# Hybrid GLA/FoX decoder block: where the split v of the GLA output step is kept, and in which order the steps of its four heads are given out

## The chip, the cores and the metric

The kernel runs on one core of one Trainium2 chip. The metric is the device time of one execution in microseconds (us). The kernel before took 1661.32 us, the median of three runs (1660.44 to 1662.15).

## The reference

One decoder layer on 256 tokens of width 2048, all in float32. Only the first part bears on the change:

```
q, k, v, r  = parts of x @ w_in            # GLA: 4 heads, dk 256, dv 512
o_t  = sum over s <= t of  A[t, s] * v_s   # A: q.k with a data-dependent decay
o    = o * rsqrt(mean(o*o) + eps) * gain   # per head, over its 512 columns
o    = o * silu(r)
y_gla = o @ w_branch_gla
```

FoX attention, two merge gates `sigmoid(x @ w)` (2048 columns each), the output projection, LayerNorm, a gated MLP, a second LayerNorm and a per-layer embedding follow or stand beside it.

## The kernel before

**Number format.** Every float32 matrix product is done as three products of rounded parts: `hi` is the operand copied by ScalarE (ACT) into the fast float32r format, `lo` is the remainder `x - hi`, subtracted by VectorE (DVE). The products hi·hi, hi·lo and lo·hi are added in PSUM. So each weight matrix costs a DMA (`raw`), an ACT copy (`hi`, L112) and a DVE subtraction (`lo`, L220) before TensorE (PE) can use it.

**Weights.** Units of 1 MB pass in a fixed order through `prep` (two DMAs on SyncE's (SP's) queue into a ring of five buffers, then `hi` and `lo`, six buffers each), three units ahead of use. SP's order is the program's order; the order on the other engines is made by a scheduler when the program is built. It places an instruction as early as its inputs and a free buffer allow.

**Stages in time.** Value and early projections (`fv`, `psfq`, `psfk`), GLA q and k and the matrices A (`at`), 20 of 32 merge-gate products (`merge_gate`, tile `psm`), the GLA values v (`gv`) and the output gate r (`gr`) by `s_half`, then the remaining twelve gate products n = 20 to 31, and then the branch products (`psa` with the GLA output `oT`, `psb` with FoX). Each gate product is 16 pairs of products: 512 columns with `hi` (L287) and 256 with `lo` (L289).

**The GLA output step.** `o_gen` is a generator whose pieces are given out between the products of those twelve gates: from n = 21 on, `pull(1)` is called after the pairs 3 and 11 of each gate. For each head h it does

- `split(h)`: v is split into hi and lo (tile `vs`, 8 KB per partition, taken from the pool of fifteen 8 KB buffers, `s8`), and A into `ath` and `atl`;
- `product(h)`: nine products of 512 columns (L956) into two PSUM banks (`go`), the sum of squares on ACT (L959), the power -0.5 on GpSimd (POOL, L963), and the scaled and gated result `og` on DVE (L965);
- `turn(h)`: eight transposes of `og` on PE (L974, tile `gt`, the same two PSUM banks, pool `pmx`), then their split into the 8 KB tile `oT` (ACT L112, DVE L992).

Between the pieces stand yields, and the heads follow one another:

```
for h in range(H):
    split(h); yield; yield
    product(h); yield; yield
    turn(h); yield
```

**Buffers.** While the twelve gates run, the fifteen 8 KB buffers hold x transposed (4), the FoX output (2), A (1), the gate results (4) and v with r (4, freed head by head). `vs` and `oT` need buffers of the same pool. A second, smaller space, the pool `ec`, holds constants of the early stages (masks, a scan reset, a matrix of ones, the norm gain `gnb`); it is closed after the twelve gates. Of these only `gnb` is still used in the stage `gr` (L922).

Later tiles take the 8 KB buffers as they come free. The next is `td`, 1 MB of weights that `park_gen` loads during the branch products (L160) to prepare them ahead; its DMA stands in SP's queue between the loads of `raw`, which wait behind it.

Of the kernel before, what the change touches and what calls it, by code (L numbers as in the profile page):

```python
# [9 lines left out]
F32 = mybir.dt.float32  # L10
F32R = mybir.dt.float32r
# [3 lines left out]
ALU = mybir.AluOpType  # L15
# [4 lines left out]
P = 128  # L20
# [4 lines left out]
H = 4  # L25
# [19 lines left out]
PSM1 = 20  # L45
# [27 lines left out]
def tile_block(ctx: ExitStack, tc: tile.TileContext, wu, wfv, wpp, xT_in, x_in, pT_in, wlr,  # L73
               chan, gnorm, lng, ident_in, mask_in, cmask_in, out):
    nc = tc.nc
# [13 lines left out]
    sm = ctx.enter_context(tc.tile_pool(name="sm", bufs=2))  # L89
    early = ctx.enter_context(ExitStack())  # L90
    ec = early.enter_context(tc.tile_pool(name="ec", bufs=1))
    pmm = ctx.enter_context(tc.tile_pool(name="pmm", bufs=6, space=PSUM))
    pmx = ctx.enter_context(tc.tile_pool(name="pmx", bufs=2, space=PSUM))
    dr = ctx.enter_context(tc.tile_pool(name="dr", bufs=1, space=DRAM))

    def s8(shape, dt=F32, name=None):
        return big.tile(shape, dt, tag="S8", name=name)
# [4 lines left out]
    def t2(name):  # L102
        return sm.tile([P, 512], F32, tag="t2", bufs=6, name=name)

    def mmtile(name):
        return pmm.tile([P, 512], F32, tag="mm", name=name)

    def mxtile(name):
        return pmx.tile([P, 512], F32, tag="mx", name=name)

    def copy(o, i, scale=1.0):
        return nc.scalar.activation(o, i, AF.Copy, bias=0.0, scale=scale)  # L112
# [115 lines left out]
    def unit(ahead=3):  # L228
        u = n_used[0]
        n_used[0] += 1  # L230
        while n_prep[0] < min(NU, u + ahead):
            prep()
        return ready.pop(u)
# [19 lines left out]
    ident = cst.tile([P, P], F32, name="ident")  # L253
    mask = ec.tile([P, 8, 256], U8, name="mask")
    cmask = ec.tile([P, 256], F32, name="cmask")
    gnb = ec.tile([P, 512], F32, name="gnb")
    reset = ec.tile([P, 256], F32, name="reset")
    ones = ec.tile([P, P], F32R, name="ones")
    gSt = ec.tile([P, 256], F32R, name="gSt")
# [20 lines left out]
    def w_unit(ps, hi, lo, act, kts, first, last, hoff=0, tick=None):  # L280


        n = len(kts)
        for i, kt in enumerate(kts):
            a = act[kt // 4]
            w0 = (hoff + i) * P
            nc.tensor.matmul(ps, lhsT=hi[i // 8 if hoff == 0 else 0][:, w0 % 1024:w0 % 1024 + P],  # L287
                             rhs=a[:, kt % 4, :], start=first and i == 0, stop=False)
            nc.tensor.matmul(ps[:, 256:512],  # L289
                             lhsT=lo[i // 8 if hoff == 0 else 0][:, w0 % 1024:w0 % 1024 + P],  # L290
                             rhs=a[:, kt % 4, 0:256], start=False, stop=last and i == n - 1)
            if tick is not None:
                tick(i)
# [15 lines left out]
    def comb(ps, o, scale=1.0):  # L309
        tmp = t1("tmp")  # L310
        copy(tmp, ps[:, 256:512], scale)
        a = ps[:, 0:256]
        if len(o.shape) == 3:
            a, tmp = [v.rearrange("p (t n) -> p t n", t=2) for v in (a, tmp)]
        if scale == 1.0:
            nc.vector.tensor_tensor(o, a, tmp, ALU.add)
        else:
            nc.vector.scalar_tensor_tensor(o, a, scale, tmp, ALU.mult, ALU.add)
# [19 lines left out]
    def pull(n, gens=mixers):  # L338
        for _ in range(n):
            while gens:  # L340
                try:
                    next(gens[0])
                    break
                except StopIteration:
                    gens.pop(0)
# [92 lines left out]
    for u in range(8):  # L438
        hi, lo = fvu[u]
        for j in range(2):  # L440
# [8 lines left out]
            for t, i, c in seq:  # L449
                o, n = fch[c]  # L450
                w, x = prods[t][i]
# [34 lines left out]
    for t in range(2):  # L486
        for c, (o, n) in enumerate(fch):
            n = min(n, 1024 - o)
# [146 lines left out]
    for n in range(16):  # L635
        h, j = n // 2, n % 2
# [89 lines left out]
    for n in range(16):  # L726
        nm, dst, sc = (("q", gq, 1.0 / 16.0), ("k", gk, 1.0))[n // 2 % 2]
        h, c = n // 4, n % 2
# [157 lines left out]
    def merge_gate(n, tick=None):  # L886
        hi, lo = unit()
        ps = mmtile(f"psm{n}")
        w_unit(ps, hi, lo, xT, range(16), True, True, tick=tick)
        dst = sg[n // 8][:, n % 8, :]  # L890
        comb(ps, dst)
        nc.scalar.activation(dst, dst, AF.Tanh, bias=0.0, scale=0.5)
# [11 lines left out]
        pull(1)  # L904


    vg = [s8([P, 2, 2, 512], name=f"vg{h}") for h in range(H)]

    for nh in range(2):
# [26 lines left out]
    def o_gen():  # L936
        parts, ogs = {}, {}

        def split(h):
            vs = s8([P, 2, 2, 512], F32R, name=f"vs{h}")  # L940
            copy(vs[:, 0], vg[h][:, 0])
            nc.vector.tensor_tensor(vs[:, 1], vg[h][:, 0], vs[:, 0].bitcast(F32), ALU.subtract)
            ah, al = [sm.tile([P, 384], F32R, tag="t2", bufs=6, name=n) for n in ("ath", "atl")]
            copy(ah, at[h])
            nc.vector.tensor_tensor(al, at[h], ah.bitcast(F32), ALU.subtract)
            parts[h] = vs, ah, al

        def product(h):
            vs, ah, al = parts.pop(h)
            for t in range(2):  # L950
                po = mxtile(f"go{h}_{t}")
                ks = ((0, 0),) if t == 0 else ((256, 0), (128, 1))
                mm = [(x[:, o:o + P], vs[:, i, s, :]) for o, s in ks
                      for x, i in ((ah, 0), (ah, 1), (al, 0))]
                for j, (x, v) in enumerate(mm):
                    nc.tensor.matmul(po, lhsT=x, rhs=v, start=j == 0, stop=j == len(mm) - 1)  # L956
                sq = t2("sq")
                st = sm.tile([P, 2], F32, tag="gst", name="gst")
                nc.scalar.activation(sq, po, AF.Square, bias=0.0, scale=1.0,  # L959
                                     accum_out=st[:, 0:1])  # L960
                nc.vector.tensor_scalar(st[:, 0:1], st[:, 0:1], 1.0 / 512, RMS_EPS,
                                        ALU.mult, ALU.add)
                nc.gpsimd.tensor_tensor(st[:, 1:2], st[:, 0:1], mhalf, ALU.pow)  # L963
                og = ogs[h, t] = t2("og")
                nc.vector.scalar_tensor_tensor(og, po, st[:, 1:2], vg[h][:, 1, t, :],  # L965
                                               ALU.mult, ALU.mult)

        def turn(h):
            oT[h] = s8([P, 4, 512], F32R, name=f"oT{h}")
            for t in range(2):  # L970
                og = ogs.pop((h, t))
                pt = mxtile(f"gt{h}_{t}")
                for i in range(4):
                    nc.tensor.transpose(pt[:, i * P:i * P + P], og[:, i * P:i * P + P], ident)  # L974
                split_T(pt, oT[h], t)

        for h in range(H):
            split(h)
            yield
            yield  # L980
            product(h)
            yield
            yield
            turn(h)
            yield

    def split_T(pt, dst, t):

        p3 = pt.rearrange("p (k t) -> p k t", t=P)
        hi = dst[:, :, t * P:t * P + P]  # L990
        copy(hi, p3)
        nc.vector.tensor_tensor(dst[:, :, 256 + t * P:256 + t * P + P], p3,  # L992
                                hi.bitcast(F32), ALU.subtract)

    mixers.append(o_gen())


    for n in range(PSM1, 32):
        merge_gate(n, lambda i: pull(1) if i in (3, 11) and n > PSM1 else None)
    while mixers:  # L1000
        pull(1)
    early.close()
# [6 lines left out]
    for n in range(16):  # L1009
# [27 lines left out]
        i = WO_C.index(pair)  # L1037
# [242 lines left out]
    for n in range(NF):  # L1280
# [23 lines left out]
        if pair in DN_S[0]:  # L1304
            if j == 0:
                yp = t2("yp").rearrange("p (k t) -> p k t", t=S)
            h = yp[:, j, :]
        else:
            h = y
# [266 lines left out]
```

## Time and profile before

| | |
|---|---|
| median of three runs | 1661.32 us |
| profiled execution | 1661.22 us |
| its span (first to last instruction) | 1659.4 us |
| PE busy | 1652.1 us |
| weight loads on PE (PEld) | 1434.6 us |
| DVE busy | 1307.9 us |
| ACT busy | 899.8 us |
| POOL busy | 71.2 us |
| granted PE clock | 1.0 |

All times in the views are from the span's start. The profiled execution's time is 1.8 us longer than its span. The ends of products on PE are modelled, and products overlap; so what a product costs PE is read from its start to the start of the next one. In the view in order of time a row gives start, duration, engine, line, operation, output and inputs, the number of merged instructions, and in brackets the idle time before it with what ended it.

### The profile page before, as it was taken

How to read it: one execution, taken by the hardware profiler on the slowest of the kernel's cores; microseconds unless marked ns; L12 is line 12 of the kernel's file. 1: busy time of each engine (PE TensorE's matmuls, PEld its weight loads, DVE VectorE, ACT ScalarE, POOL GpSimd, SP SyncE). 2: the span in 40 equal slices, each digit the busy share in tenths (PEclk: the TensorE clock that was granted, in tenths of full speed). 3: DMA queues.
4: the chain of work that ended last, by engine and by line, in shares of the span. 5: the costliest groups of instructions: out<-in, count | busy, mean ns of one | idle time of the engine just before them, and what ended most of it. 6: DMA issues, size and time to landing. Idle time of an engine off the chain costs nothing.

```text
span 1659.4 us, 24382 instructions
## 1 busy us (share of the span) xinstructions
PE 1652.1 (100%) x8917; PEld 1434.6 (86%) x8917; DVE 1307.9 (79%) x1983; ACT 899.8 (54%) x1314; POOL 71.2 (4%) x210
## 2 busy tenths in 40 slices
PE   9999999999999999999999999999999999999998
PEld 9988888888888888888898888888888888888887
DVE  7666877888889767888987877777777778988774
ACT  6655555555555654455575455555545556556543
POOL 0100000000000000000010101100111000000000
PEclk9999999999999999999999999999999999999999
DMA  8755555546566556878856877778677679898554
GB/s 322 254 165 169 170 175 173 185 158 201 199 205 203 186 187 250 307 241 306 314 172 204 274 269 268 265 243 290 241 263 253 237 268 339 288 363 312 177 187 156
DMA packets 103432, 391.61 MB, mean 236 GB/s; under 512 B 11736, under 2 KB 13024, under 8 KB 96400
## 3 DMA queue, kind: packets, MB, share of 16 engines
q1 hardware_dynamic: 98448, 363.83, 64.3%
q0 software_dynamic: 4864, 26.23, 4.2%
q8 instruction: 70, 1.15, 0.3%
q14 instruction: 50, 0.41, 0.1%
HBM read 362.74 MB, written 27.27 MB: 235 GB/s over the span
## 4 chain that ended last, share of the span: by engine, by line
PE 98%; DVE 1%; ACT 0%; issue 0%; POOL 0%; POOLq 0%; DVEq 0%; ACTq 0%
PE dn L792 10%; PE psu L287 10%; PE psg L287 9%; PE psm L287 7%; PE pg L333 5%; PE psu L289 5%; PE psg L289 5%; PE gv L792 4%; PE gr L792 4%; PE wo L792 4%; PE psm L289 4%; PE dn_p L792 3%; PE psa L287 3%; PE fv L452 3%; PE psfk L287 2%; PE psk L287 2%
## 5 line engine op out<-in xcount | busy, mean ns | idle before, releaser
L220 DVE TENSOR_TENSOR lo<-raw,hi 128x1024 fp32r<-128x1024 f32 x490 | 595.0, 1220 | 192.8 <-ACT hi L112 190.7
L112 ACT ACTIVATE hi<-raw 128x1024 fp32r<-128x1024 f32 x490 | 516.0, 1057 | 380.3 <-issue 143.5
L287 PE MATMUL psu<-x1T,hi 128*128 128x512 f32 x688 | 240.4, 392 | 0.0
L287 PE MATMUL psg<-x1T,hi 128*128 128x512 f32 x672 | 234.8, 392 | 0.0
L289 PE MATMUL psu<-x1T,lo 128*128 128x256 f32 x688 | 192.3, 280 | 0.0
L289 PE MATMUL psg<-x1T,lo 128*128 128x256 f32 x672 | 187.8, 280 | 0.0
L287 PE MATMUL psm<-xT,hi 128*128 128x512 f32 x512 | 181.4, 396 | 0.0
L287 PEld LDWEIGHTS psu<-x1T,hi 128*128 128x128 f32 x688 | 129.2, 188 | 27.6
L287 PEld LDWEIGHTS psg<-x1T,hi 128*128 128x128 f32 x672 | 126.2, 188 | 27.0
L289 PE MATMUL psm<-xT,lo 128*128 128x256 f32 x512 | 143.3, 280 | 0.0
L289 PEld LDWEIGHTS psu<-x1T,lo 128*128 128x128 f32 x688 | 130.6, 190 | 0.0
L289 PEld LDWEIGHTS psg<-x1T,lo 128*128 128x128 f32 x672 | 127.6, 190 | 0.0
L287 PEld LDWEIGHTS psm<-xT,hi 128*128 128x128 f32 x512 | 96.2, 188 | 19.7
L792 PE MATMUL dn<-hi,hC 128*128 128x512 f32 x368 | 102.3, 389 | 0.0
L289 PEld LDWEIGHTS psm<-xT,lo 128*128 128x128 f32 x512 | 97.1, 190 | 0.2
L112 ACT ACTIVATE hi_b<-raw 128x512 fp32r<-128x512 f32 x78 | 65.3, 841 | 53.5 <-DMA raw<-in_wu_dram 19.8
L112 ACT ACTIVATE hi_t<-raw 128x1024 fp32r<-128x1024 f32 x48 | 51.0, 1063 | 75.5 <-DVE raw L148 51.1
L287 PE MATMUL psa<-oT,hi 128*128 128x512 f32 x256 | 89.8, 392 | 0.0
L194 DVE TENSOR_TENSOR lo_b<-raw,hi_b 128x512 fp32r<-128x512 f32 x78 | 73.7, 952 | 15.4 <-ACT hi_b L112 15.3
L792 PEld LDWEIGHTS dn<-hi,hC 128*128 128x128 f32 x368 | 69.0, 188 | 14.4
L289 PE MATMUL psa<-oT,lo 128*128 128x256 f32 x256 | 71.6, 280 | 0.0
L333 PE MATMUL pg<-hi,x2T 128*128 128x512 f32 (+1 forms) x256 | 69.7, 380 | 0.0
(366 smaller groups left out, 3199.5 us busy)
## 6 DMA issues: line engine op xcount, KB each, us to landing
raw<-in_wu_dram SPq DMA_DIRECT2D x553, 512.0 KB, 5.1
td<-in_wu_dram SPq DMA_DIRECT2D x15, 1024.0 KB, 8.5
td<-td POOLq DMA_DIRECT2D x15, 1024.0 KB, 6.5
td<-td SPq DMA_DIRECT2D x15, 1024.0 KB, 8.2
hS<-sd SPq DMA_DIRECT2D x21, 512.0 KB, 8.2
fvraw<-in_wfv_dram SPq DMA_DIRECT2D x13, 524.0 KB, 6.6
sd<-hs POOLq DMA_DIRECT2D x24, 256.0 KB, 5.7
lnb<-in_lng_dram SPq DMA_DIRECT2D x4, 1024.0 KB, 10.3
```

What stands on the lines that cost most here:

```text
L112: return nc.scalar.activation(o, i, AF.Copy, bias=0.0, scale=scale)
L194: nc.vector.tensor_tensor(lo, src, hi.bitcast(F32), ALU.subtract)
L220: i = nc.vector.tensor_tensor(lo, raw, hi.bitcast(F32), ALU.subtract)
L287: nc.tensor.matmul(ps, lhsT=hi[i // 8 if hoff == 0 else 0][:, w0 % 1024:w0 % 1024 + P], rhs=a[:, kt % 4, :], start=first and i == 0, stop= ...
L289: nc.tensor.matmul(ps[:, 256:512], lhsT=lo[i // 8 if hoff == 0 else 0][:, w0 % 1024:w0 % 1024 + P], rhs=a[:, kt % 4, 0:256], start=False, ...
L333: nc.tensor.matmul(bs[j][:, 0:m], lhsT=x, rhs=v[:, o:o + m], start=first and i == 0, stop=last and i == 2)
L452: nc.tensor.matmul(fbk[t][c][:, 0:n], lhsT=x, rhs=w[:, o:o + n], start=kt == 0 and i == 0, stop=kt == 15 and i == 2)
L792: nc.tensor.matmul(ps, lhsT=x, rhs=w, start=todo[id(ps)] == total[id(ps)], stop=todo[id(ps)] == 1)
```

## The change

- The pool `ec` first holds `gnb` alone. All other early constants go to a second pool, `ec2`, in the space behind it, and this pool is closed before the values stage; a third pool, `ec3`, is opened in the same space.
- `split(h)` no longer takes an 8 KB buffer. The hi part of v (`vh`, 4 KB) and one half of its lo part (`vl`, 2 KB) lie in `ec3`, in one buffer each; the other half of the lo part lies in a 2 KB buffer of the ring `t2` (six buffers, which `ath`, `atl`, `og` and the squares use too). The subtraction is made in two instructions of 512 columns instead of one of 1024.
- The order of the pieces: a new head begins every four pulls, its product two pulls after its split, and its transposes three pulls after its product (before: every five pulls, two, and two). The transposes of a head thus come after the split of the next one.
- The condition of the pulls is written in another way and holds for the same gates and pairs.

```diff
     ec = early.enter_context(tc.tile_pool(name="ec", bufs=1))
+    gnb = ec.tile([P, 512], F32, name="gnb")
+    first_ = ctx.enter_context(ExitStack())
+    ec = first_.enter_context(tc.tile_pool(name="ec2", bufs=1))
...
-    gnb = ec.tile([P, 512], F32, name="gnb")
...
+    first_.close()
+    ec = early.enter_context(tc.tile_pool(name="ec3", bufs=1))
     vg = [s8([P, 2, 2, 512], name=f"vg{h}") for h in range(H)]
...
         def split(h):
-            vs = s8([P, 2, 2, 512], F32R, name=f"vs{h}")
-            copy(vs[:, 0], vg[h][:, 0])
-            nc.vector.tensor_tensor(vs[:, 1], vg[h][:, 0], vs[:, 0].bitcast(F32), ALU.subtract)
+            vh = ec.tile([P, 2, 512], F32R, tag="vh", name=f"vh{h}")
+            copy(vh, vg[h][:, 0])
+            vl = [ec.tile([P, 512], F32R, tag="vl", name=f"vl{h}"),
+                  sm.tile([P, 512], F32R, tag="t2", bufs=6, name="vl1")]
+            for t in range(2):
+                nc.vector.tensor_tensor(vl[t], vg[h][:, 0, t], vh[:, t].bitcast(F32),
+                                        ALU.subtract)
+            vs = [(vh[:, t], vl[t]) for t in range(2)]
...
-                mm = [(x[:, o:o + P], vs[:, i, s, :]) for o, s in ks
+                mm = [(x[:, o:o + P], vs[s][i]) for o, s in ks
...
-        for h in range(H):
-            split(h)
-            yield
-            yield
-            product(h)
-            yield
-            yield
-            turn(h)
+        for k in range(19):
+            for f, o in ((turn, 5), (product, 2), (split, 0)):
+                h, r = divmod(k - o, 4)
+                if r == 0 and 0 <= h < H:
+                    f(h)
             yield
...
-        merge_gate(n, lambda i: pull(1) if i in (3, 11) and n > PSM1 else None)
+        merge_gate(n, lambda i: pull(1) if i in (3, 11) and 2 * n + i // 8 > 2 * PSM1 + 1 else None)
```

## The prediction

> **What bounds the kernel now.** I read the page's busy times first, then who waited for whom on PE, then PE's order of time where those waits lie.
>
> ```profile
> PE 1652.1 (100%) x8917; PEld 1434.6 (86%) x8917; DVE 1307.9 (79%) x1983; ACT 899.8 (54%) x1314; POOL 71.2 (4%) x210
> ```
>
> PE is busy in all but 7.3 us of the span of 1659.4. So the number of PE instructions and PE's waits set the time; work on DVE or ACT counts only where PE waits for it. The whole list of PE's waits has four rows (us in total, times, longest):
>
> ```profile
> PE warm_ps L122 <- DVE warm L119: 1.2, 1, 1.2
> PE gt L974 <- DVE og L965: 0.7, 2, 0.4
> PE gt L974 <- DVE gst L961: 0.4, 1, 0.4
> PE go L956 <- DVE atl L945: 0.4, 1, 0.4
> ```
>
> The first is the start of the program. The other three belong to the GLA output step: 1.5 us in four places. That understates the loss, since the modelled end of a product reaches past the start of the next. I therefore count from start to start. What an undisturbed product takes:
>
> ```profile
> 551.90 0.39 PE L287 MATMUL psm<-xT,hi 128*128 128x512 f32 x1
> 552.13 0.28 PE L289 MATMUL psm<-xT,lo 128*128 128x256 f32 x1
> 552.25 0.40 PE L287 MATMUL psm<-xT,hi 128*128 128x512 f32 x1
> ```
>
> 0.23 us for 512 columns, 0.12 for 256; a pair of a gate product takes 0.35, a gate of 16 pairs 5.55. Against that, the places where PE stood:
>
> ```profile
> 549.12 0.63 PE L956 MATMUL go<-vs,ath 128*128 128x512 f32 x2
> 550.18 0.50 PE L956 MATMUL go<-vs,atl 128*128 128x512 f32 x1 [0.43 <-DVE atl L945]
> 550.52 0.62 PE L956 MATMUL go<-vs,ath 128*128 128x512 f32 x2
> ...
> 607.00 0.73 PE L956 MATMUL go<-vs,ath 128*128 128x512 f32 x2
> 607.56 0.28 PE L289 MATMUL psm<-xT,lo 128*128 128x256 f32 x1
> ...
> 610.68 0.40 PE L287 MATMUL psm<-xT,hi 128*128 128x512 f32 x1
> 611.51 0.66 PE L974 MATMUL gt<-ident,og 128*128 128x128 f32 x4 [0.43 <-DVE gst L961]
> ...
> 612.36 0.28 PE L289 MATMUL psm<-xT,lo 128*128 128x256 f32 x1
> 613.05 0.66 PE L974 MATMUL gt<-ident,og 128*128 128x128 f32 x4 [0.41 <-DVE og L965]
> ...
> 619.70 0.39 PE L287 MATMUL psa<-oT,hi 128*128 128x512 f32 x1
> 620.39 0.66 PE L974 MATMUL gt<-ident,og 128*128 128x128 f32 x4 [0.30 <-DVE og L965]
> ```
>
> Head 0 at 549.12: two products took 1.06 instead of 0.45 and the next 0.34 instead of 0.23, together **0.72 lost**. Heads 2 and 3: 0.83 - 0.23 = 0.60, 0.69 - 0.12 = 0.57 and 0.69 - 0.23 = 0.46, together **1.63 lost**. At 607.00 the products of head 2 are torn apart: 0.56 instead of 0.45, **0.11 lost**. Each return from transposes to products costs a little too:
>
> ```profile
> 557.45 1.04 PE L974 MATMUL gt<-ident,og 128*128 128x128 f32 x8
> 558.24 0.48 PE L287 MATMUL psm<-xT,hi 128*128 128x512 f32 x1
> 558.56 0.28 PE L289 MATMUL psm<-xT,lo 128*128 128x256 f32 x1
> ```
>
> 0.32 instead of 0.23, so 0.09. Heads 0 and 1 return once each, heads 2 and 3 twice each, because their transposes come in fours: six returns. Everything the change can win on PE lies in these lines; behind them PE has no gap:
>
> ```profile
> 622.06:750.00 127.94, 127.94 (x741) 113.13 (x740) 105.27 (x177) 62.53 (x95) 2.72 (x5) 1.00 0.75 268
> ```
>
> (stretch, length, then the busy time of PE first.) So what is won before 622 stays won, if nothing new makes PE wait.
>
> **Why heads 2 and 3 are late.** By the pulls, split 2 is given out in gate n = 26 and split 3 in n = 28. The trace has them here (ACT, then DVE, then the results):
>
> ```profile
> 605.88 1.06 ACT L112 ACTIVATE vs<-vg 128x1024 fp32r<-128x1024 f32 x1
> ...
> 607.00 1.21 DVE L942 TENSOR_TENSOR vs<-vg,vs 128x1024 fp32r<-128x1024 f32 x1
> ...
> 610.70 0.75 DVE L965 SCALAR_TENSOR_TENSOR og<-go,gst,vg 128x512 f32<-128x512 f32 x1 [0.73 <-POOL gst L963]
> ```
>
> The gates begin at 536.64 (the end of the last `gr` product) and take 5.55 us each; a head costs PE nine products at 0.23, eight transposes in 0.79 (557.45 to 558.24) and the return, 3.0 together. With two heads done, n = 31 begins at 536.64 + 11 x 5.55 + 2 x 3.0 = 603.7, so split 2 stands in the last gate. Neither engine was too busy for it: what was missing is the 8 KB buffer, which came free only when the last gate had read the first part of x. After that the chain product, square, power, `og`, transposes, `oT` has only the rest of one gate and the first branch product beside it, and PE waits.
>
> **The change, part by part.**
>
> *Split v out of the 8 KB pool: heads 2 and 3.* `vh` and half of `vl` take the space of constants that were last read before the values stage; that space is free from then on. Each has one buffer, so split h+1 waits for product h; by the new order it stands two pulls, one gate, behind it. All four products and transposes then lie between gates n = 22 and n = 29 with gates beside them, and the three waits of 1.63 and the torn product of 0.11 go. Four whole groups of transposes return four times instead of six: 0.18 less. **Sum -1.92.**
>
> *What is late next for a head:* its `og`. Product to transposes is now three pulls, at least 8.3 us. In the trace head 2's products ended near 610, its `og` began at 610.70, and the transposes that waited for the second half began at 613.05: about 3 us are needed. Covered.
>
> *The split subtraction.* One instruction of 1024 columns becomes two of 512:
>
> ```profile
> L942 DVE TENSOR_TENSOR vs<-vg,vs 128x1024 fp32r<-128x1024 f32 x4 | 4.9, 1218 | 0.5 <-ACT vs L112 0.5
> L928 DVE TENSOR_TENSOR vg<-vg,gr 128x512 f32<-128x512 f32 x4 | 2.5, 679 | 0.0
> ```
>
> 2 x 679 - 1218 = 140 ns more on DVE per head, 0.56 us in all, beside PE work: 0, except for head 0 (next). The Trainium skill, "VectorE: DVE Perf Modes", section "The TRN2 errata — SBUF-src ops pay a fixed extra latency per instruction", speaks against this edit: a large tile pays the fixed part once, small ones each time. Its formula (N + 151)/0.96 gives 691 and 1224 ns, so an estimate of 158 ns more per head; the rows agree within some 20 ns, and by page or row the sum is the same.
>
> *Head 0's wait, now 0.72.* Its product stands where it stood (pull 2, 549.12). It needs `atl`, the last of a row of DVE work, and in the changed program one half of `vl` stands directly before `atl`, 0.61 us from start to start for such an instruction. Against that the whole `vs` of head 0 leaves DVE's queue before it, since `vh` and the first half of `vl` can be made right after the values stage:
>
> ```profile
> 518.40 1.22 DVE L942 TENSOR_TENSOR vs<-vg,vs 128x1024 fp32r<-128x1024 f32 x1
> ...
> 523.16 1.23 DVE L194 TENSOR_TENSOR lo_t<-raw,hi_t 128x1024 fp32r<-128x1024 f32 x1 [1.21 <-ACT hi_t L112]
> ...
> 531.15 1.23 DVE L220 TENSOR_TENSOR lo<-raw,hi 128x1024 fp32r<-128x1024 f32 x1 [1.62 <-ACT hi L112]
> ...
> 535.22 3.49 DVE L220 TENSOR_TENSOR lo<-raw,hi 128x1024 fp32r<-128x1024 f32 x3
> 538.63 2.47 DVE L928 TENSOR_TENSOR vg<-vg,gr 128x512 f32<-128x512 f32 x4
> ...
> 549.58 0.54 DVE L945 TENSOR_TENSOR atl<-at,ath 128x384 fp32r<-128x384 f32 x1
> ```
>
> From 538.63 to 549.58 DVE has no idle time (the bracket is empty in every row between), so `atl` moves as the row of 538.63 does. That row could have begun near 536.6, when the last `gr` products ended, but three subtractions lay ahead. They wait for weights: the transfers reuse the ring buffers that the subtraction at 523.16 and those after it free, and that one waited for ACT, which waited for DVE's differences behind `vs`. Without the 1.1 us that `vs` takes from the next start, this chain moves forward by 1.1 or more (its two waits for ACT can shrink as well), and at most by 2.0 (538.63 - 536.64). Needed for no wait: `atl` done by 549.57 (the start of the third product) instead of 550.18, with 0.61 more ahead of it: 1.22. Bounds: with no shift the wait grows to 0.72 + 0.61 = 1.33; with a shift of 1.22 or more it is 0. I take 0, because the shift's range is 1.1 to 2.0 and the remainder at its low end is 0.1. **-0.72.** By the page's 691 ns for that half, the need would be 1.30 instead of 1.22.
>
> *The early half.* `vh` (1.05 on ACT) and `vl` (0.68 on DVE) now run at the end of the first values half, among weight preparation. If they delayed a weight, PE would lose at most those 1.05; but units are prepared up to three ahead, a unit is 21 or 24 products of 0.23 there, about 5 us, and PE's list of waits has none in that stage. I take 0.
>
> *SP's queue.* The buffers of the later tiles change hands in another order. The first `td` waited for the last `atl` and left at
>
> ```profile
> 613.84 0.33 SPq L160 DMA_DIRECT2D td<-in_wu_dram  x1
> 617.28 0.33 SPq L216 DMA_DIRECT2D raw<-in_wu_dram  x1
> ```
>
> Now it waits for PE's reading of the first quarter of x in gate n = 31: that gate begins at 536.64 + 11 x 5.55 + 4 x 3.0 = 609.7, and four pairs later it is 611. The weight behind `td` left at 617.28, for reasons of its own ring. No new wait: 0. DMAs in number and size, and the work of ACT and POOL, are unchanged: 0.
>
> **Sum:** -1.92 - 0.72 = -2.6 of the profiled execution's 1661.22 (1.8 of it outside the span): 1658.6. The median is 0.1 above that execution, so **1658.7**. One can't tell less than about 0.2% (3.3 us) from no change with this kernel; the forecast is a gain below that.
>
> **Rivals.**
>
> *Head 0 still waits* (no shift in DVE's chain, or `ath` late): the wait is 0.6 to 1.33, and the time 1659.3 to 1660.0. For it: each link of the chain must pass the shift on, and the first link is a transfer. Chance 0.16.
>
> *The two PSUM banks become the wait; slower than before.* `go` and `gt` share two banks. Product h+1 now follows the transposes of head h after eight pairs, 2.8 us; before it was three pulls. From the start of the transposes that is 0.8 + 2.8 = 3.6 us, and by then ACT and DVE must have emptied the first bank, behind whatever subtraction of 1.2 us is at work:
>
> ```profile
> 558.72 1.29 DVE L992 TENSOR_TENSOR oT<-gt,oT 128x512 fp32r<-128x512 f32 x2
> ```
>
> That is done at 560.0, 2.6 after the start at 557.45, and there DVE had a subtraction and a gate sum ahead. Three heads are exposed. Each 1.2 us subtraction more makes it 3.8, so two more give 5.0, a wait of 1.4 at three places, 4.2: 1658.7 + 4.2 = 1662.9, slower than before. It decides from an emptying 4.5 us after the start on. Chance 0.05, of which 0.03 for over 0.2%.
>
> *The step is not spread* (the scheduler or another buffer, of `t2` or `oT`, holds the last heads back): 1661.3. `oT` does take an 8 KB buffer per head, but product h frees v's. Chance 0.04.
>
> *Faster than the waits allow:* by the count above no more than about 3 us is there, so 1657.8 needs the scatter between runs, 1.7 us wide here. Chance 0.10.
>
> **How the numbers follow.** The forecast has 0.65, its own range is 1658.0 to 1659.3. Below 1658.0 (faster by over 0.2%) lie the last rival and a little of the forecast's edge: 0.13. Slower by over 0.2%: 0.03. Within: 0.84. The range of 1657.7 to 1660.4 takes in the forecast, head 0's wait with its upper bound, and most of the scatter below; it leaves out the shared banks, the step not spread, and some scatter.
>
> **What would show it.** Right: PE's waits keep only the start's 1.2; transposes in groups of eight at four places, all before psa begins near 615; `atl` of head 0 done before 549.6; span near 1656.8. Wrong: a wait of `go` on `atl` above 0.4 (head 0), a wait of `go` on `oT` (banks), products of head 3 in or behind gate n = 31 (not spread), or a new wait of PE for a weight between 400 and 540 or behind 615 (a cover that I took as given).

## The result, and the profile after

The changed kernel takes 1658.59 us (median; 1657.78 to 1659.58), the kernel before 1661.28 in the same series (1660.3 to 1662.85): ratio 0.9984, 95% interval 0.9978 to 0.9991. That is 2.69 us less, below the 0.2% that the prediction set as the bound of "no change". The changed kernel's profiled span is 1656.7 us, against 1659.4.

The busy times of the page, and the whole list of PE's waits (us in total, times, longest), after the change:

```profile
PE 1651.0 (100%) x8917; PEld 1435.0 (87%) x8917; DVE 1310.1 (79%) x1987; ACT 900.2 (54%) x1314; POOL 70.7 (4%) x210
```

```profile
PE warm_ps L125 <- DVE warm L122: 1.2, 1, 1.2
```

PE has as many instructions as before, DVE four more (the split subtraction) and 2.2 us more work; two more profiles of each kernel (experiments 7 to 10) have 1308.8 and 1308.3 before, 1309.3 and 1309.6 after, so on the mean it is 1.3 more, and the rest is scatter. Only the start of the program is left as a wait; the three rows of the GLA output step are gone. PE in order of time after the change, at head 0's products, at head 0's transposes, at the first products of heads 2 and 3, at head 3's transposes, and where the gates end:

```profile
549.06 0.39 PE L965 MATMUL go<-vh,ath 128*128 128x512 f32 x1
549.30 0.39 PE L965 MATMUL go<-vl,ath 128*128 128x512 f32 x1
549.53 0.39 PE L965 MATMUL go<-vh,atl 128*128 128x512 f32 x1
549.76 0.39 PE L965 MATMUL go<-vh,ath 128*128 128x512 f32 x1
...
559.49 1.03 PE L983 MATMUL gt<-ident,og 128*128 128x128 f32 x8
560.28 0.48 PE L289 MATMUL psm<-xT,hi 128*128 128x512 f32 x1
560.60 0.28 PE L291 MATMUL psm<-xT,lo 128*128 128x256 f32 x1
...
577.24 0.39 PE L965 MATMUL go<-vh,ath 128*128 128x512 f32 x1
...
591.32 0.39 PE L965 MATMUL go<-vh,ath 128*128 128x512 f32 x1
...
601.75 1.04 PE L983 MATMUL gt<-ident,og 128*128 128x128 f32 x8
602.54 0.48 PE L289 MATMUL psm<-xT,hi 128*128 128x512 f32 x1
...
615.00 0.28 PE L291 MATMUL psm<-xT,lo 128*128 128x256 f32 x1
615.12 0.39 PE L289 MATMUL psa<-oT,hi 128*128 128x512 f32 x1
```

Head 0's nine products step by 0.23 without a break. Head 2's products begin at 577.24 instead of 607.00, and its v is split 40 us earlier (ACT, at 605.88 before):

```profile
566.09 1.05 ACT L115 ACTIVATE vh<-vg 128x1024 fp32r<-128x1024 f32 x1
```

Transposes come in groups of eight, the last at 601.75, 13 us before the gates end (before: those of heads 2 and 3 in groups of four, up to 620.39, behind the gates), and each group costs only the return of 0.09. Counted from start to start between 536 and 660 us, PE lost 3.07 us before and 0.34 after: 2.73 gone, the difference of the two profiled spans. Behind it PE is as full as before (stretch, length, then PE's busy time first):

```profile
618.00:746.00 128.00, 128.00 (x740) 113.19 (x739) 105.10 (x174) 63.06 (x96) 2.71 (x5) 1.00 0.79 280
```

So the two profiles agree with the forecast to 0.1 us. The experiments show that one of its terms was nevertheless wrong.

### The profile page after: what moved, and what is told of

The parts are those of the page before. It is cut to its first block, busy times and chain, and to the rows that moved or that the text cites. A ratio compares the mean times of both kernels' runs of the same rounds, so it can differ in the third digit from the quotient of the medians.

```text
span 1656.7 us, 24388 instructions
## 1 busy us (share of the span) xinstructions
PE 1651.0 (100%) x8917; PEld 1435.0 (87%) x8917; DVE 1310.1 (79%) x1987; ACT 900.2 (54%) x1314; POOL 70.7 (4%) x210
## 4 chain that ended last, share of the span: by engine, by line
PE 99%; DVE 0%; ACT 0%; POOL 0%; issue 0%
PE dn L794 10%; PE psu L289 10%; PE psg L289 9%; PE psm L289 7%; PE pg L335 5%; PE psu L291 5%; PE psg L291 5%; PE gv L794 4%; PE gr L794 4%; PE wo L794 4%; PE psm L291 4%; PE psa L289 4%; PE dn_p L794 3%; PE fv L454 3%; PE psa L291 2%; PE psfk L289 2%
```

## The experiments

### 1. The order alone, v in the 8 KB pool as before

The edit, made to the kernel before:

```diff
-        for h in range(H):
-            split(h)
-            yield
-            yield
-            product(h)
-            yield
-            yield
-            turn(h)
+        for k in range(19):
+            for f, o in ((turn, 5), (product, 2), (split, 0)):
+                h, r = divmod(k - o, 4)
+                if r == 0 and 0 <= h < H:
+                    f(h)
             yield
```

> The kernel before with the new order of the pieces alone (a head every four pulls, transposes three pulls behind the product); the split v stays in the 8 KB pool. Theory (the missing 8 KB buffer holds heads 2 and 3 back, not the order): product 2 still falls in gate n = 31 and head 3 behind it; head 0's wait stays near 0.7 and the waits of heads 2 and 3 stay near 1.6 or grow, since three pulls between product and transposes mean nothing when all is late; about 1661.3 us, within 1.5. Rival (the order spreads the heads): products 2 and 3 at 587 and 593 us as in the changed kernel, about 1659.3.

Measured: 1661.04 us, ratio 1.0002 (0.9993 to 1.0011). PE's waits at the GLA step, and in order of time the place where they lie:

```profile
PE gt L974 <- DVE og L965: 0.7, 2, 0.5
PE gt L974 <- DVE gst L961: 0.4, 1, 0.4
```

```profile
606.62 0.40 PE L287 MATMUL psm<-xT,hi 128*128 128x512 f32 x1
606.95 0.73 PE L956 MATMUL go<-vs,ath 128*128 128x512 f32 x2
...
613.34 0.66 PE L974 MATMUL gt<-ident,og 128*128 128x128 f32 x4 [0.54 <-DVE og L965]
...
615.93 0.62 PE L956 MATMUL go<-vs,ath 128*128 128x512 f32 x2
...
619.28 0.66 PE L974 MATMUL gt<-ident,og 128*128 128x128 f32 x4 [0.43 <-DVE gst L961]
```

The pieces are given out earlier, but product 2 still runs in the last gate and product 3 behind it. The order brings nothing by itself. The second finding is a miss: there is no wait for `atl`, though this kernel splits v exactly as before does, and my prediction had hung head 0's wait on that split.

### 2. The buffer alone, heads in the old order

The edit above, reversed, made to the changed kernel.

> The changed kernel with the old order of the pieces (a head every five pulls, transposes two pulls behind the product); the split v lies in the space of the early constants. Theory (the buffer alone does it): all four products and transposes lie in the gates up to n = 30, PE waits for none of them, PE's loss between 536 and 660 us is 0.4 as in the changed kernel, about 1658.6 us. Rival (the overlap or the longer distance of the transposes is needed): PE waits for og or gst before transposes at up to four places, 0.3 to 0.6 each, 1659 to 1661.

Measured: 1658.73 us, ratio 0.9986 (0.9978 to 0.9995). PE's list keeps only the start; PE lost 0.48 between 536 and 660 (0.34 as in the changed kernel, and 0.14 at head 0's products). The new place of v alone makes the whole gain, so the 8 KB buffer was what heads 2 and 3 waited for. The chain of experiment 1 failed at the same buffer, whatever the order.

### 3. Only head 0's v in the new space

Made to the changed kernel in the old order; heads 1 to 3 take the 8 KB buffer again:

```diff
         def split(h):
+            if h > 0:
+                v8 = s8([P, 2, 2, 512], F32R, name=f"vs{h}")
+                copy(v8[:, 0], vg[h][:, 0])
+                nc.vector.tensor_tensor(v8[:, 1], vg[h][:, 0], v8[:, 0].bitcast(F32), ALU.subtract)
+                vs = [(v8[:, 0, t], v8[:, 1, t]) for t in range(2)]
...
+                parts[h] = vs, ah, al
+                return
```

> The old order, and only head 0's split v in the space of the early constants (with its early half after the values stage); heads 1 to 3 split v in the 8 KB pool as before. Theory (the two gains are separate: head 0's comes from the subtraction taken out of VectorE's queue during the r stage, that of heads 2 and 3 from the buffer): PE's wait for the lo part of A at 549 us goes (0.7), the waits of heads 2 and 3 stay (about 1.6 to 1.9); about 1660.6 us. Rival (both gains have the buffer as cause): the heads move up or head 0's wait stays: 1658.6 or 1661.3.

Measured: 1660.66 us, ratio 0.9998 (0.999 to 1.0007). The waits at the GLA step, and DVE ahead of head 0's product:

```profile
PE gt L993 <- DVE og L984: 0.7, 2, 0.4
PE gt L993 <- DVE gst L980: 0.4, 1, 0.4
PE go L975 <- DVE atl L964: 0.4, 1, 0.4
```

```profile
537.83 2.48 DVE L932 TENSOR_TENSOR vg<-vg,gr 128x512 f32<-128x512 f32 x4
...
548.77 0.70 DVE L959 TENSOR_TENSOR vl<-vg,vh 128x512 fp32r<-128x512 f32 x1
549.37 0.57 DVE L964 TENSOR_TENSOR atl<-at,ath 128x384 fp32r<-128x384 f32 x1
```

Heads 2 and 3 wait as before: that half is as expected. Head 0's wait should have gone and stayed (0.66 from start to start). Experiments 1 and 3 together turn the prediction's step round: with the old split no wait, with the new one a wait.

### 4. One more subtraction on DVE in the r stage

Made to the changed kernel; nothing reads the result of the added instruction:

```diff
+        if u == 81:
+            for i in range(1):
+                nc.vector.tensor_tensor(t2("idle"), vg[0][:, 0, i], r0[:, 0:512], ALU.subtract)
```

> The changed kernel with one extra subtraction of 128x512 on VectorE, its result unused, in the r stage at the place where the kernel before subtracted head 0's v (it also puts a weight subtraction between the two differences, as before). Theory (head 0's wait is set by how early VectorE's chain starts the sums at 537 us): that start moves back from 537.09 by 0.6 to 1.5, the lo part of A is done at 549.8 to 550.7, PE waits 0.2 to 1.1 us before the third product of head 0 and nowhere else; 1658.8 to 1659.7 us. Rival (ScalarE's hi part of A or the early half sets it): no wait, 1658.6.

Measured: 1659.13 us, ratio 0.9989 (0.998 to 0.9998). Head 0's wait is back, 0.56 from start to start:

```profile
PE go L968 <- DVE atl L957: 0.3, 1, 0.3
```

The size is as expected, but with what the repeats below show, one execution can't tell the added 0.69 us from scatter.

### 5. Transposes two pulls behind the product, as before

```diff
-            for f, o in ((turn, 5), (product, 2), (split, 0)):
+            for f, o in ((turn, 4), (product, 2), (split, 0)):
```

> The changed kernel with the transposes two pulls behind their product, as before, instead of three; a head still begins every four pulls. Theory (two pulls, 5.5 us, cover the about 3 us from the end of the product to the second half of og): no wait of PE, the same loss of 0.4 between 536 and 660 us, about 1658.6 us. Rival (the longer distance is a part of the gain): PE waits for og before transposes, up to four times 0.3 to 0.6, 1659 to 1661.

Measured: 1658.40 us, ratio 0.9983 (0.9974 to 0.9992), no wait in the GLA step, PE's loss 0.33. The greater distance between product and transposes brings nothing: once v is not late, two pulls cover the chain to `og`. It can't be told from the changed kernel (1658.59), so it isn't a better version either.

### 6. Transposes directly ahead of the next product

The rival of the two PSUM banks, made as tight as the pulls allow:

```diff
-        for k in range(19):
-            for f, o in ((turn, 5), (product, 2), (split, 0)):
+        for k in range(20):
+            for f, o in ((turn, 6), (product, 2), (split, 0)):
```

> The changed kernel with the transposes of a head four pulls behind their product, which puts them directly in front of the next head's product. Theory (products and transposes share two PSUM banks, and a bank is empty some 1.9 and 2.6 us after the start of the transposes): PE stands before the next product at three places, about 1.0 to 1.7 us each, 3 to 5 us in all: 1661.5 to 1663.7 us, slower than before. Rival (the emptying is quick or the scheduler fills the gap with gate products): 1658.6 to 1659.5.

Measured: 1659.40 us, ratio 0.999 (0.9981 to 0.9999). One of the three places:

```profile
562.57 1.03 PE L983 MATMUL gt<-ident,og 128*128 128x128 f32 x8
563.36 0.48 PE L289 MATMUL psm<-xT,hi 128*128 128x512 f32 x1
...
564.38 0.28 PE L291 MATMUL psm<-xT,lo 128*128 128x256 f32 x1
564.62 0.50 PE L965 MATMUL go<-vh,ath 128*128 128x512 f32 x1
564.96 0.39 PE L965 MATMUL go<-vl,ath 128*128 128x512 f32 x1
```

The scheduler put three gate pairs between the transposes and the product. The product began 564.62 - 562.57 = 2.05 us after the transposes, 0.12 late, and cost 0.34 instead of 0.23: 0.23 at this place and at the second, 0.18 at the third, instead of the 1.0 and more that I expected of it. The mechanism is there (the weight load in front of this product waited 0.28 for DVE's `oT`), but the first bank was empty about 2 us after the start, and the prediction's rival needed 4.5. The other 0.32 of this run stand at head 0's product.

### 7 and 8. The kernel before, profiled twice more

No edit. After experiments 1 and 3 the question was whether head 0's wait belongs to the program or to one execution.

> The kernel before, profiled once more, to see how far head 0's wait differs between two executions of one program. Scatter theory (the landing of r's weight tiles decides, and differs from execution to execution; the order-only kernel has before's split on DVE and started its sums at 537.48 with no wait): the start of the four sums of vg with gr, 538.63 in the trace of before, moves by more than 0.3 us, and head 0's wait is anywhere from 0 to 1.1. Queue theory (my prediction: the split subtraction of head 0 in DVE's queue near 518 sets it): the sums start within 0.2 of 538.63 and head 0's wait is 0.5 to 0.8 again.

> The kernel before a third time. Scatter theory: the start of the sums differs from that of the second profile of before by more than 0.2, and where it starts by 537.5 there is no wait at head 0, as in the order-only kernel. Queue theory: within 0.2 of 538.63, head 0's wait 0.5 to 0.8. In both: the waits of heads 2 and 3 (0.7, 0.7 and 0.4) are there again within 0.1 each.

Measured: 1660.30 and 1660.62 us. The second profile of before, its whole list of PE's waits, then DVE:

```profile
PE warm_ps L122 <- DVE warm L119: 1.2, 1, 1.2
PE gt L974 <- DVE og L965: 0.7, 2, 0.4
PE gt L974 <- DVE gst L961: 0.4, 1, 0.4
```

```profile
537.09 2.48 DVE L928 TENSOR_TENSOR vg<-vg,gr 128x512 f32<-128x512 f32 x4
...
548.03 0.55 DVE L945 TENSOR_TENSOR atl<-at,ath 128x384 fp32r<-128x384 f32 x1
```

And the third profile of before:

```profile
538.05 2.48 DVE L928 TENSOR_TENSOR vg<-vg,gr 128x512 f32<-128x512 f32 x4
...
549.00 0.55 DVE L945 TENSOR_TENSOR atl<-at,ath 128x384 fp32r<-128x384 f32 x1
```

One program: the sums begin at 538.63, 537.09 and 538.05, `atl` at 549.58, 548.03 and 549.00, and the wait for `atl` is there in the first only. The waits of heads 2 and 3 are the same in all three. The scatter theory holds; the queue theory, which was the prediction's, falls. ACT's order of time in the first and the second profile of before shows where they part, at a copy that waited for a weight's landing:

```profile
526.83 0.58 ACT L112 ACTIVATE vg<-gr_p 128x512 f32<-128x512 f32 x1
530.06 1.06 ACT L112 ACTIVATE hi<-raw 128x1024 fp32r<-128x1024 f32 x1 [2.66 <-DMA raw<-in_wu_dram]
```

```profile
526.22 0.58 ACT L112 ACTIVATE vg<-gr_p 128x512 f32<-128x512 f32 x1
528.04 1.06 ACT L112 ACTIVATE hi<-raw 128x1024 fp32r<-128x1024 f32 x1 [1.25 <-DMA raw<-in_wu_dram]
```

The row ahead of it lies 0.61 apart in the two, the copy itself 2.02.

### 9 and 10. The changed kernel, profiled twice more

> The changed kernel, profiled once more. Scatter theory: the start of the sums of vg with gr (537.09 in its first trace) moves by more than 0.2, up to 538.0, and when it is later than about 537.5 a wait of head 0's first product of up to 0.6 is back, since vl stands ahead of atl on DVE. Queue theory: 537.0 to 537.3 and no wait. In both: no wait at heads 2 and 3, four returns of about 0.09.

> The changed kernel a third time. Scatter theory: the start of the sums between 537.0 and 538.0, differing from the other two profiles of it by more than 0.2 at least once, with a wait at head 0 wherever atl ends after PE is ready for it. Queue theory: 537.0 to 537.3, no wait at head 0. In both: no wait at heads 2 and 3.

Measured: 1659.20 and 1658.88 us; no wait at heads 0, 2 and 3 in either, four returns of 0.09. The sums began at 537.14 and 537.25, `atl` at 548.69 and 548.80. From the span's start that is within 0.2 of the first profile's 537.09, as the queue theory had it and not as the scatter theory expected. Counted from a mark on PE (the 75 `gv` products, below) the three profiles stand up to 0.5 apart. More scatter showed up where the same split ran in other orders: 537.22 in experiment 5, 537.50 in 2, 537.58 in 6, 537.83 in 3.

## Why the prediction was right or wrong

**Heads 2 and 3: right in mechanism and nearly in size.** The forecast was -1.92. The cleanest measure lies between two marks on PE, in the chain of work that ended last: from a run of 75 `gv` products in the values stage to one of 99 `dn` products in the last stage (start, duration). First the kernel before in its second profile, then the changed kernel in its first:

```profile
400.47 17.00 PE gv L792 x75
...
1425.97 22.44 PE dn L792 x99
```

```profile
400.75 17.00 PE gv L794 x75
...
1424.18 22.44 PE dn L794 x99
```

That is 1025.50 and 1023.43. The third profile of before has 1025.50 too; the second and third of the changed kernel have 1023.63 (with 0.15 lost at 1389, far behind the change) and 1023.48. So without head 0's wait the change is worth **1.9 to 2.1 us**. From start to start, the second profile of before has 0.60 + 0.58 + 0.46 at heads 2 and 3, 0.12 at the torn product, 0.16 for two more returns and 0.07 ahead of head 3's first transposes: 1.99. Experiments 1 and 2 show that the buffer did it and not the order.

**Head 0: the step that failed.** The prediction took -0.72, "because the shift's range is 1.1 to 2.0" once `vs` leaves DVE's queue. The sums did begin 1.54 earlier in the changed kernel's first profile. But the kernel before, unchanged, began them 1.54 earlier as well, in its second profile. The first profile of before was the late one, and I priced its accident as a property of the program. What decides is when `atl` begins. Counted from the start of the 75 `gv` products, with PE's loss at head 0's products:

| | sums begin | `atl` begins | loss |
|---|---|---|---|
| before, 1st profile | 137.85 | 148.80 | 0.72 |
| 3: only head 0 in the new space | 137.18 | 148.72 | 0.66 |
| 4: one more subtraction | 137.16 | 148.70 | 0.56 |
| 6: transposes ahead of the next product | 136.84 | 148.39 | 0.32 |
| 2: buffer alone | 136.66 | 148.20 | 0.14 |
| before, 3rd profile | 137.17 | 148.12 | 0.04 |
| changed, 1st profile | 136.34 | 147.88 | 0 |
| changed, 3rd profile | 136.14 | 147.69 | 0 |
| 5: transposes two pulls behind | 136.08 | 147.63 | 0 |
| before, 2nd profile | 136.62 | 147.56 | 0 |
| changed, 2nd profile | 135.84 | 147.39 | 0 |
| 1: order alone | 136.44 | 147.38 | 0 |

From about 148.1 on PE loses time, below it does not, whichever split is used. With the old split (before three times, and experiment 1) the sums begin at 137.02 on the mean, with the new one (the changed kernel three times, 2, 3, 5, 6) at 136.44: perhaps 0.6 earlier, within scatters of 1.4 and 1.3. But `vl` then stands ahead of `atl` with its 0.60, and `atl` begins at 147.97 and 147.99 on the mean; the losses are 0.19 and 0.16. So the prediction had both parts of this step, the shift and the 0.61, but on these means the shift is no larger than what `vl` takes back: head 0's term is about 0, not -0.72. Eleven profiles can't exclude a few tenths: in the three of before `atl` begins at 148.16 on the mean, in the three of the changed kernel at 147.65, with losses of 0.25 and 0. Nor can they separate executions from chips: experiments 1 to 4, 5 and 6, and 7 to 10 ran on three chips, and for the first two profiles the chip isn't recorded. On one chip (7 and 8) the sums of one program still began 0.55 apart.

**Where the shift went.** The prediction let the chain through SP's ring of buffers pass the shift on whole. ACT in the changed kernel's first profile, to be set beside the rows of 526.83 and 530.06 in experiments 7 and 8:

```profile
523.68 0.58 ACT L115 ACTIVATE vg<-gr_p 128x512 f32<-128x512 f32 x1
...
528.52 1.06 ACT L115 ACTIVATE hi<-raw 128x1024 fp32r<-128x1024 f32 x1 [2.72 <-DMA raw<-in_wu_dram]
```

The row ahead moved by 3.15, the copy that waits for the weight by 1.54. That weight's DMA was issued at 524.42 and took 5.5 us to land before; it was issued at 522.22 and took 6.2 after. On the means of the same eleven profiles, counted from the 75 `gv` products, the issue stands at 123.42 with the old split and 121.72 with the new one, the landing at 128.22 and 127.70. So the shift was there at the issue, 1.7, and 0.5 of it was left at the landing: this is the link that failed. The prediction's rival for head 0 had named it ("the first link is a transfer"), with a chance of 0.16. Why the earlier transfer takes longer stays open.

**Why the time came out all the same.** The change is worth about 2.0 where head 0 doesn't wait, 2.7 where only the kernel before waits. The medians differ by 2.69, with an interval from 1.5 to 3.7 us that holds both. Experiments 2 and 5, whose traces show nearly all and all of the gain, came to 2.02 and 2.64 below their own runs of before. How often either kernel waits at head 0, and so how much of the other 0.6 is real, stays open. The forecast was worked out from the one late profile of before, so that it met the median to 0.1 us is in part luck. A forecast without head 0's term would have been 1661.3 - 1.92 = 1659.4, inside the range as well.

**The banks (rival).** Priced at 1.4 a place; forced in experiment 6, they cost 0.18 to 0.23. In the changed kernel product h+1 begins 563.15 - 559.49 = 3.66 after the transposes, as the prediction had it (3.6), and finds the banks free.

**What I took at nothing.** The split subtraction, the early half of `vl` and SP's queue brought no wait in any list of the GLA step or the values stage. DVE's half of `vl` takes what its neighbour rows led me to take (679 ns; three figures: shortest, median, longest):

```profile
L949 DVE TENSOR_TENSOR vl<-vg,vh x8: 681/683/687, 416.3 to 582.6; 128x512 fp32r<-128x512 f32 x8
```

The Trainium skill, "VectorE: DVE Perf Modes", section "The TRN2 errata — SBUF-src ops pay a fixed extra latency per instruction", gives 691 by its formula; the trace agrees within 8 ns. `td` was forecast for about 611 and left at 615.41, right behind a `raw` of 615.04 in SP's queue; the weight behind it left 0.3 later than before (617.28), and nobody waited:

```profile
615.41 0.98 SPq L163 DMA_DIRECT2D td<-in_wu_dram  x1
617.59 5.88 SPq L219 DMA_DIRECT2D raw<-in_wu_dram  x3
```

**The other two parts of the change** move the pieces but not the time: the overlap of neighbouring heads (experiment 2 has the old order and the whole gain), and the transposes further behind their product (experiment 5).

## What to carry to other kernels

When a step runs late though its engines have room, look for the buffer that it has to wait for before changing the order: here the order alone gave 0, the buffer alone everything. A wait of half a microsecond that hangs on the landing of a transfer may belong to one execution; profile the unchanged kernel a second time before pricing it, and compare stretches between two marks on PE (here 75 `gv` and 99 `dn` products), which repeat to 0.2 us where spans scatter by 0.9. A shift that has to pass through a transfer should be followed to the landing: here 1.7 us at the issue left 0.5.

## What the runs showed of the hardware

- After PE has stood for an operand, the next product steps by 0.34 instead of 0.23, so each stall costs about 0.11 beyond the wait: seen at head 0 in the kernel before and in experiments 2, 3, 4 and 6, and at the banks in 6. Experiment 4's list of waits shows 0.28 for a loss of 0.56.
- One weight tile took 5.5, 4.1 and 5.0 us from issue to landing in the three profiles of the kernel before (the copies at 530.06 and 528.04 belong to the first two), and 6.2, 5.8 and 5.8 in the three of the changed kernel, where it was issued 2.0 us earlier on the mean.
- The start of the program up to the values stage scatters too: the 75 `gv` products begin between 400.47 and 401.30. The third profile of the changed kernel waits 0.5 us there (`fv` for ACT's `xT`), which has nothing to do with the change.
